# A matmul with rotary embedding: earlier first stores, half of the middle stores on another queue, two more block pairs, and a slice of the multiplication on GpSimd

## The chip, the core and the metric

The kernel runs on one core of a Trainium2 chip. A core has five engines with a queue of instructions each: TensorE (PE; PEld is its weight load), VectorE (DVE), ScalarE (ACT), GpSimd (POOL) and SyncE (SP), which only issues DMAs. Here SyncE and ScalarE issue DMAs. Matmul results go to PSUM, eight banks of 128 x 512 fp32; everything else is in SBUF. The metric is the device time of one execution in microseconds.

## What is computed

The reference, cut to what matters (batch 16, sequence 512, hidden 768, 12 heads of 64):

```
y = np.matmul(x, weight)                      # (16, 512, 768) x (768, 768)
y = y.reshape(16, 512, 12, 64)
y1, y2 = y[..., :32], y[..., 32:]
out1 = y1 * cos[..., :32] - y2 * sin[..., :32]
out2 = y2 * cos[..., 32:] + y1 * sin[..., 32:]
out = np.concatenate([out1, out2], axis=-1).reshape(16, 512, 768)
```

All arrays are float32. The kernel multiplies in fp16 with fp32 sums.

## The kernel before

**Tiles and groups.** The 8192 rows of x are 64 tiles of 128 rows; tile i has one batch and every fourth row of it. Four tiles with the same residue r of the row number are a group g (16 groups, 0 to 15), so that one piece of cos and sin serves the whole group. The results of a group are 4 x 768 = 3072 columns, which fill six PSUM banks (`py`). A tile needs 6 chunks of 128 along the contraction, and its 768 columns lie in two banks (one piece of 512, one of 256), so it takes 12 matmuls (L291).

**How x is turned.** A matmul needs x with the contraction on the partitions. There are two ways. A *turned* tile is loaded (`load`, 384 KB, rows of 3072 bytes), cast to fp16 by ScalarE (`cast`, `xc<-xs`), transposed by six TensorE transposes (L232) into a PSUM tile `pt`, and copied to SBUF by ScalarE (`xt<-pt`). A *pair* (two neighbouring tiles, listed in `BLOCKS`) is loaded so that 32 x 32 blocks lie right (four quarters of 192 KB, in pieces of 768 bytes: two quarters are issued by SyncE, two by ScalarE), cast by ScalarE (`cast_pair`, `xd<-xb`) and transposed by one VectorE instruction (L252). Before the change, the second halves of groups 3 to 14 and the first halves of groups 5, 7, 9, 11 and 13 are pairs, 17 in all; 30 tiles are turned. Pair buffers: `NB` is 4.

**The rotary part.** A *unit* is 1024 columns of a group (three units; smaller ones in the last two groups). VectorE multiplies the unit in PSUM by cos and by the swapped and signed sin at once, into `tq` (L309, output 2 x 1024). GpSimd adds the two products, the second with its halves exchanged, into the output buffer `ov` (L320). `tq` has five buffers (two of them in the space of the raw weights, named `w_raw` in the profile), `ov` has four, one a group. `store` (L341) writes half a group (768 KB).

**The order of the work.** The order on every engine is written out by hand; semaphores are placed by `Flow.do` from the buffers that an instruction reads and writes. After tile i's matmuls the loop from L510 calls, in this order: `bturns` (VectorE transposes of pairs that begin fewer than 6 tiles ahead; fewer before tile 8), `turns` (TensorE transposes and ScalarE's copy of a tile that is 3 ahead), `casts` (ScalarE's casts up to 7 tiles ahead; 4 before tile 8, and at tile 8 the casts of tiles 12 to 15 at once), and then a store if one is due. Inside `casts`, after each cast, `pump` gives SyncE the next loads whose buffers are free by then, and ScalarE gets at most one quarter of a pair, of a pair at most `LEAD` = 12 tiles ahead and only if a pair buffer is counted free:

```
                if n < xb_used[0] + NB and i >= g * QB + 2 * h - LEAD:
                    load_quarter(pairs[n], 2 + q, "act")
```

Store k (0 or 1) of group o is issued after tile 4(o+2) + 2k for groups 0 to 10, so after tiles 8, 10, 12, 14, 16, 18 for the first three groups; nearly all by ScalarE, from group 13 on by SyncE. DMAs are issued by a queue's owner in order with its other instructions: what stands behind an issue on ScalarE waits until it is done.

Of the kernel before, what the change touches and what calls it, by code (L numbers as in the profile page):

```python
# [10 lines left out]
FP32 = mybir.dt.float32  # L11
FP16 = mybir.dt.float16
MULT = mybir.AluOpType.mult
ADD = mybir.AluOpType.add


class Flow:
# [24 lines left out]
    def do(self, e, make, reads=(), writes=(), dma=None, tick=True):  # L42
        need = {}
        for k in reads:
            for s, v in self.wrote.get(k, {}).items():
                need[s] = max(need.get(s, 0), v)
        for k in writes:
            for d in (self.wrote, self.readby):
                for s, v in d.get(k, {}).items():
                    need[s] = max(need.get(s, 0), v)  # L50
        if e == "pe":
            need.pop("pe", None)
        waits = self.settle(e, need)
        for s, v in waits[:-1]:
            self.eng[e].wait_ge(self.sem(s), v)  # L55
        i = make(self.eng[e])
        if waits:
            s, v = waits[-1]
            i.wait_op(self.sem(s), v, "sem-ge")
        name, step = (dma, 16) if dma else (e, 1)  # L60
        self.sem(name)
        at = self.count[name] + step
        if tick or dma:
            i.then_inc(self.sems[name], step)
            self.count[name] = at
            self.known[name, at] = dict(self.seen[e])
        for k in reads:
            d = self.readby.setdefault(k, {})
            d[name] = max(d.get(name, 0), at)
        for k in writes:  # L70
            self.wrote[k] = {name: at}
            self.readby[k] = {}
        return i
# [30 lines left out]
def kernel(  # L104
# [11 lines left out]
    f = Flow(nc, tc)  # L116
    do = f.do
    P = nc.NUM_PARTITIONS

    B, S, H = x.shape  # L120
    NH = int(n_heads)
    D = H // NH
# [5 lines left out]
    QB = 4  # L128
# [3 lines left out]
    LAST = NG - 1  # L132


    BLOCKS = {(g, 1) for g in range(3, 15)} | {(g, 0) for g in (5, 7, 9, 11, 13)}

    def sbuf(name, shape, dt):
        return nc.alloc_sbuf_tensor(name, shape, dt).ap()

    NX, NB, NC, NCP, NXT, NXP, NTQ, NOV = 11, 4, 5, 2, 8, 4, 3, 4  # L140

    ident = sbuf("ident", [P, P], FP16)
    cold = sbuf("cold", [P, 512], FP16)
# [1 line left out]
    csn = sbuf("csn", [P, 2, SB, D], FP32)  # L145
# [8 lines left out]
    tq_b = [sbuf(f"tq{i}", [P, 2, 1024], FP32) for i in range(NTQ)]  # L154
    w_flat = w_raw.rearrange("p t e n -> p (t e n)")
    tq_b += [w_flat[:, ts(i, 2048)].rearrange("p (j n) -> p j n", j=2) for i in range(2)]
    W_HOME = [f"wr{t}{h}" for t, h in CHUNKS]
    ov_b = [sbuf(f"ov{i}", [P, QB * H], FP32) for i in range(NOV)]
    py = nc.alloc_psum_tensor("py", [P, 6 * 512], FP32).ap()
# [2 lines left out]
    def ring(name, n, state={}):  # L162
        k = state.get((id(f), name), 0)
        state[id(f), name] = k + 1
        return k % n

    def copy(e, o, i_):
        return lambda eng: (
            eng.copy(out=o, in_=i_) if e == "act" else eng.tensor_copy(out=o, in_=i_)  # L169
        )  # L170

    def where(i):
        g, s = divmod(i, QB)
        return QB * (g // SB) + s, g % SB

    def pair_of(i):
        return i // QB, (i % QB) // 2

    def is_block(i):
        return pair_of(i) in BLOCKS  # L180

# [112 lines left out]

    ov_of = {}

    late = []

    def rope(g, u):
        c0, c1, ps, banks, adder = u  # L300
        w, r = c1 - c0, g % SB
        nh = w // D
        if adder == "dve":
            k = len(late)
            tq, keys = xs_b[k][:, 0 : 2 * w].rearrange("p (j n) -> p j n", j=2), [f"xs{k}"]
        else:
            k = ring("tq", NTQ + 2)
            tq, keys = tq_b[k][:, :, 0:w], [f"tq{k}"] + (W_HOME if k >= NTQ else [])
        do("dve", lambda eng: eng.tensor_tensor(  # L309
            out=tq.rearrange("p j (h d) -> p j h d", d=D),  # L310
            in0=ps.rearrange("p (h d) -> p h d", d=D)
            .unsqueeze(1).broadcast_to((P, 2, nh, D)),
            in1=csn[:, :, r, :].unsqueeze(2).broadcast_to((P, 2, nh, D)),
            op=MULT), reads=banks + ["csn"], writes=keys)
        if g not in ov_of:
            ov_of[g] = ring("ov", NOV)
        o = ov_of[g]

        def add():
            do(adder, lambda eng: eng.tensor_tensor(  # L320
                out=ov_b[o][:, ds(c0, w)].rearrange("p (h t d) -> p h t d", t=2, d=HD),
                in0=tq[:, 0].rearrange("p (h t d) -> p h t d", t=2, d=HD),
                in1=tq[:, 1].rearrange("p (h t d) -> p h t d", t=2, d=HD)[:, :, ::-1, :],
                op=ADD), reads=keys[:1], writes=[f"ov{o}c{c}" for c in range(c0, c1, 64)])

        if adder == "dve":
            late.append(add)
        else:
            add()

    def store(g, c0, c1, e):

        o = ov_of[g]
        b, r = where(g * QB)
        s0, s1 = c0 // H, -(-c1 // H)
        dst = out.rearrange("b (p r) h -> r p b h", r=SB)[r, :, b + s0 : b + s1]
        src = ov_b[o].rearrange("p (b h) -> p b h", b=QB)[:, s0:s1]
        if (c1 - c0) % H:
            dst = dst[:, 0, c0 - s0 * H : c1 - s0 * H]
            src = src[:, 0, c0 - s0 * H : c1 - s0 * H]  # L340
        do(e, lambda eng: eng.dma_start(out=dst, in_=src),  # L341
           reads=[f"ov{o}c{c}" for c in range(c0, c1, 64)], dma=f"ov{o}_{c0}")
# [5 lines left out]
        out=ident, in_=ident, compare_op=mybir.AluOpType.not_equal, fill=1.0,  # L348
# [3 lines left out]
    for k in order:  # L352
# [5 lines left out]
        out=csn[:, 0], in_=cos.rearrange("(p r) d -> p r d", r=SB)), writes=["cos"], dma="cos")  # L358
    do("sp", lambda eng: eng.dma_start(
        out=sin_sb, in_=sin.rearrange("(p r) d -> p r d", r=SB)), writes=["sin"], dma="sin")  # L360


    want = [(i, i) for i in range(QB, NTILE) if not is_block(i)]
    for g, h in BLOCKS:
        want += [(g * QB + 2 * h - 2.5 + 3 * q, ((g, h), q)) for q in (0, 1)]
# [41 lines left out]
    def castx(i, e):  # L407
        cast(i, e)
        xs_used[0] += 1
# [22 lines left out]
    for c in CHUNKS[3:5]:  # L432
# [5 lines left out]
        out=csn[:, 1, :, 0:HD], in_=sin_sb[:, :, HD:D]), reads=["sin"], writes=["csn1"])  # L438
    do("dve", lambda eng: eng.tensor_scalar_mul(
        out=csn[:, 1, :, HD:D], in0=sin_sb[:, :, 0:HD], scalar1=-1.0),  # L440
        reads=["sin", "csn1", "cos"], writes=["csn"])
    pump()

    state = {"cast": 4, "turn": 4, "bturn": 0, "half": 0}
    pairs = sorted(BLOCKS)

    def casts(upto):
        while state["cast"] < min(upto, NTILE):
            i = state["cast"]
            state["cast"] += 1  # L450
            if not is_block(i):
                castx(i, "act")
            elif i % 2 == 0:
                cast_pair(pair_of(i))
                xb_used[0] += 1
            pump()
            if state["half"] < 2 * len(pairs):
                n, q = divmod(state["half"], 2)
                g, h = pairs[n]
                if n < xb_used[0] + NB and i >= g * QB + 2 * h - LEAD:  # L460
                    load_quarter(pairs[n], 2 + q, "act")
                    state["half"] += 1
# [31 lines left out]
    for c in CHUNKS[3:]:  # L494
        mm0(3, c)
    rope(0, U0[2])
    turns(6)

    STORES = {}
    for o in range(LAST):  # L500
        for k in (0, 1):
            if o < LAST - 4:
                at = QB * (o + 2) + 2 * k
            elif o < LAST - 2:
                at = QB * (LAST - 2) + 2 * (o - LAST + 4) + k
            else:
                at = QB * (o + 1) + 2 * k
            STORES[at] = (o, k)

    for i in range(QB, NTILE):  # L510
        g, s = divmod(i, QB)
        us = units(g)
        done_to = (s + 1) * H
        for p in pieces(g, s):
            a, z, _, bank = p
            for c in CHUNKS:
                mm_piece(i, p, c, c == CHUNKS[0], c == CHUNKS[-1],
                         tick=c == CHUNKS[-1])
            for u in us:
                if u[1] == z:  # L520
                    rope(g, u)
        bturns(i + (B_AHEAD if i >= SETTLED else 3))
        turns(i + 1 + (T_AHEAD if i > QB + 1 else 2))
        casts(i + 1 + (C_AHEAD if i >= SETTLED else 3 if i == QB else 4))
        if i in STORES:
            o, k = STORES[i]
            store(o, 2 * H * k, 2 * H * (k + 1), "sp" if o > LAST - 3 else "act")
        if g == LAST:
            if s == 2:
                store(g, 0, H, "sp")  # L530
            if s == 3:
                store(g, H, 2 * H, "act")
# [3 lines left out]
    for k, add in enumerate(late):  # L536
        c = 3 * H + 256 * k
# [38 lines left out]
```

## Time and profile before

| | |
|---|---|
| median of three runs | 151.27 us (150.74 to 152.22) |
| the profiled execution | 151.62 us, span 149.8 us |
| TensorE busy | 141.2 us, 94% of the span |
| VectorE busy | 128.7 us, 86% |
| GpSimd busy | 112.8 us, 75% |
| ScalarE busy | 74.9 us, 50% |
| moved by DMA | 53.11 MB, mean 355 GB/s |
| stores issued by ScalarE | 26 of 768 KB, median 13.7 us to landing |

A group's line in the profile has: line, engine, operation, output and input with shapes, number of instructions, then busy microseconds and the mean in nanoseconds, then the idle time of the engine before them and what ended it. A line of the chain in order of time has the start, the duration, and the work. A line of a timeline has the start, the duration, engine and line, and in brackets the engine's idle time before and what released it; "ACTq" is ScalarE's sequencer, which issues DMAs. The span is the program's own time on the core; the execution's time is 1.8 us longer.

### The profile page before, as it was taken

The page shows a single profiled execution, that of the slowest core. Times are in us where ns is not written, and L with a number is a line of the kernel's source. Part 1 is how long each engine was busy: PE and PEld are TensorE (multiplying, and loading weights), DVE is VectorE, ACT ScalarE, POOL GpSimd, SP SyncE. Part 2 cuts the span into 40 slices and gives each one's busy share as a digit, 9 for nine tenths or more (in the row PEclk, how much of TensorE's full clock was granted, in tenths as well). Part 3 has the DMA queues.
Part 4 walks back from the last instruction along what each step waited for, and adds up shares of the span by engine and source line. Part 5 has one row for each costly group of instructions (what it writes and reads, how often), then busy time and mean ns, then how long its engine had stood idle before and what let it go on. Part 6 is the DMA issues. An engine that isn't in the chain of part 4 may idle for free.

```text
span 149.8 us, 2471 instructions
## 1 busy us (share of the span) xinstructions
PE 141.2 (94%) x972; PEld 87.7 (59%) x972; DVE 128.7 (86%) x88; ACT 74.9 (50%) x76; POOL 112.8 (75%) x60
## 2 busy tenths in 40 slices
PE   6969999999999999999999999999999999999950
PEld 2435666666676655555666667565565666676730
DVE  0154999677999999999989999899989999998890
ACT  3444768886963280843563545444696118342100
POOL 1000299966897789887989889878988698999970
PEclk9999999999999999999999999999999999999995
DMA  4999999999999999999999999999999999997574
GB/s 129 346 400 399 404 348 293 287 297 260 227 323 399 390 373 384 388 386 387 389 382 396 391 395 396 398 385 395 399 410 410 418 413 417 396 403 311 229 278 152
DMA packets 33147, 53.11 MB, mean 355 GB/s; under 512 B 2288, under 2 KB 20464, under 8 KB 33136
## 3 DMA queue, kind: packets, MB, share of 16 engines
q10 hardware_dynamic: 16752, 27.79, 50.5%
q1 hardware_dynamic: 16384, 25.17, 48.7%
q8 instruction: 7, 0.11, 0.3%
q14 instruction: 4, 0.03, 0.1%
HBM read 27.79 MB, written 25.17 MB: 353 GB/s over the span
## 4 chain that ended last, share of the span: by engine, by line
PE 86%; DMA 5%; DVE 3%; SPq 1%; ACT 1%; issue 1%; ACTq 0%; DVEq 0%
PE py L291 80%; PE pt L232 6%; DMA w_raw<-in_weight_dram 5%; DVE xs L309 1%; ACT xc L169 1%; SPq L189 1%; DVE ov L320 1%; SPq L208 1%; DVE w_raw L309 0%; DVE w_sb L169 0%; ACTq L201 0%; DVE tq L309 0%; ACT xt L169 0%; DVEq L55 0%; SPq L571 0%
## 5 line engine op out<-in xcount | busy, mean ns | idle before, releaser
L320 POOL TENSOR_TENSOR ov<-tq 128x1024 f32<-128x1024 f32 (+2 forms) x33 | 69.0, 2107 | 27.4 <-DVE tq L309 25.7
L291 PE MATMUL py<-w_sb,xp 128*128 128x512 f16 (+1 forms) x408 | 69.4, 326 | 0.0
L309 DVE TENSOR_TENSOR tq<-py,csn 128x2048 f32<-128x2048 f32 (+2 forms) x33 | 65.8, 2015 | 3.8 <-PE py L291 3.5
L291 PE MATMUL py<-w_sb,xt 128*128 128x256 f16 (+1 forms) x360 | 60.8, 323 | 1.4 <-DVE w_sb L169 1.3
L291 PEld LDWEIGHTS py<-w_sb,xp 128*128 128x128 f16 x408 | 39.3, 98 | 24.6
L291 PEld LDWEIGHTS py<-w_sb,xt 128*128 128x128 f16 x360 | 34.2, 98 | 22.8 <-DVE w_sb L169 2.8
L320 POOL TENSOR_TENSOR ov<-w_raw 128x1024 f32<-128x1024 f32 (+2 forms) x21 | 43.6, 2087 | 4.2 <-DVE w_raw L309 4.2
L309 DVE TENSOR_TENSOR w_raw<-py,csn 128x2048 f32<-128x2048 f32 (+2 forms) x21 | 41.9, 1997 | 2.4 <-PE py L291 1.9
L169 ACT COPY xt<-pt 128x768 f16<-128x768 f16 x28 | 22.3, 800 | 31.9 <-PE pt L232 21.7
L169 ACT CAST xc<-xs 128x768 f16<-128x768 f32 x30 | 26.2, 905 | 17.7 <-issue 10.2
L169 ACT CAST xd<-xb 128x1536 f16<-128x1536 f32 x17 | 27.6, 1625 | 13.8 <-issue 5.0
L252 DVE STREAM_TRANSPOSE xp<-xd 128x768 f32<-128x768 f32 x17 | 16.4, 964 | 0.9 <-ACT xd L169 0.9
L232 PE MATMUL pt<-ident,xc 128*128 128x128 f16 x180 | 15.3, 222 | 0.2 <-ACT xc L169 0.2
L232 PEld LDWEIGHTS pt<-ident,xc 128*128 128x128 f16 x180 | 12.5, 99 | 5.2 <-ACT xc L169 1.8
L394 PE MATMUL py<-cold 128*128 128x512 f16 x12 | 5.3, 614 | 1.4 <-DVE cold L345 1.4
L169 DVE CAST w_sb<-w_raw 128x768 f16<-128x768 f32 x6 | 3.4, 558 | 3.5 <-DMA w_raw<-in_weight_dram 3.5
L169 DVE COPY xt<-pt 128x768 f16<-128x768 f16 x2 | 1.1, 558 | 5.6 <-PE pt L232 5.6
L394 PEld LDWEIGHTS py<-cold 128*128 128x128 f16 x12 | 1.6, 144 | 3.6 <-issue 2.2
L169 ACT ACT_TABLE_LOAD x1 | 1.3, 1283 | 0.9 <-SPq L114 0.9
L291 PE MATMUL pt<-w_sb,xt 128*128 128x256 f16 x12 | 1.5, 272 | 0.0
L309 DVE TENSOR_TENSOR xs<-pt,csn 128x512 f32<-128x512 f32 x2 | 1.3, 680 | 0.0
L291 PEld LDWEIGHTS pt<-w_sb,xt 128*128 128x128 f16 x12 | 1.2, 98 | 0.1
(11 smaller groups left out, 3.4 us busy)
## 6 DMA issues: line engine op xcount, KB each, us to landing
out_dram<-ov ACTq DMA_DIRECT2D x26, 768.0 KB, 13.7
xs<-in_x_dram SPq DMA_DIRECT2D x30, 384.0 KB, 9.8
xb<-in_x_dram SPq DMA_DIRECT2D x34, 192.0 KB, 8.2
xb<-in_x_dram ACTq DMA_DIRECT2D x34, 192.0 KB, 10.2
out_dram<-ov SPq DMA_DIRECT2D x4, 768.0 KB, 5.1
w_raw<-in_weight_dram SPq DMA_DIRECT2D x6, 384.0 KB, 7.5
out_dram<-ov SPq DMA_DIRECT2D x1, 384.0 KB, 2.3
out_dram<-ov ACTq DMA_DIRECT2D x1, 384.0 KB, 2.3
```

The lines of the kernel that those rows point to most:

```text
L169: eng.copy(out=o, in_=i_) if e == "act" else eng.tensor_copy(out=o, in_=i_)
L189: do(e, lambda eng: eng.dma_start(out=xs_b[k], in_=x[b].rearrange("(p r) h -> r p h", r=SB)[r]), writes=[f"xs{k}"], dma=f"xs{k}")
L208: do(e, lambda eng: eng.dma_start(out=w_raw[:, t, h], in_=wv[t, h]), writes=[f"wr{t}{h}"], dma=f"w{t}{h}")
L232: do("pe", lambda eng: eng.transpose(pt[:, t, h, :], src[:, t, h, :], ident), reads=[f"xc{c}", "ident"], writes=[f"pt{k}"], tick=(t, h) == ...
L252: do("dve", lambda eng: eng.transpose(out=dst, in_=src), reads=rd, writes=[f"xp{z}"])
L291: do("pe", lambda eng: eng.matmul(ps, get(t, h), w_sb[:, t, h, a - s * H : z - s * H], start=start, stop=stop), reads=[key, f"w{t}{h}"], w ...
L309: do("dve", lambda eng: eng.tensor_tensor(out=tq.rearrange("p j (h d) -> p j h d", d=D), in0=ps.rearrange("p (h d) -> p h d", d=D) .unsque ...
L320: do(adder, lambda eng: eng.tensor_tensor(out=ov_b[o][:, ds(c0, w)].rearrange("p (h t d) -> p h t d", t=2, d=HD), in0=tq[:, 0].rearrange(" ...
L394: do("pe", lambda eng: eng.matmul(py[:, ts(b, 512)], cold[:, 0:P], cold, start=True, stop=warmed[0] < WARM - 6), reads=["cold"], writes=[f ...
```

## The change

- `BLOCKS` gains (6, 0) and (10, 0): tiles 24, 25, 40 and 41 are loaded, cast and transposed as pairs. There are 19 pairs, and 26 turned tiles.
- `NB` becomes 5. So the halves of pair (6, 0) that ScalarE issues come after the casts of tiles 12 and 13.
- In groups 3 to 9, VectorE multiplies only the first 896 columns of the third unit. After the tile's other work (`held`), ScalarE copies the last 128 columns from PSUM to a small buffer `yb`, GpSimd multiplies them, and then does the unit's addition.
- Stores of groups 0 to 10 are issued after tile 4(o+1) + 2k + min(4, 1+o): for the first three groups after tiles 5, 7, 10, 12, 15 and 17; from group 3 on as before.
- The second stores of groups 2 to 8 are issued by SyncE.

```
-    BLOCKS = {(g, 1) for g in range(3, 15)} | {(g, 0) for g in (5, 7, 9, 11, 13)}
+    BLOCKS = {(g, 1) for g in range(3, 15)} | {(g, 0) for g in (5, 6, 7, 9, 10, 11, 13)}
...
-    NX, NB, NC, NCP, NXT, NXP, NTQ, NOV = 11, 4, 5, 2, 8, 4, 3, 4
+    NX, NB, NC, NCP, NXT, NXP, NTQ, NOV = 11, 5, 5, 2, 8, 4, 3, 4
+    PART = 128
...
+    yb_b = [sbuf(f"yb{i}", [P, PART], FP32) for i in range(2)]
...
+        def times(e, y, a, z, rd, wr):
+            n = (z - a) // D
+            do(e, lambda eng: eng.tensor_tensor(
+                out=tq[:, :, a:z].rearrange("p j (h d) -> p j h d", d=D),
+                in0=y.rearrange("p (h d) -> p h d", d=D)
+                .unsqueeze(1).broadcast_to((P, 2, n, D)),
+                in1=csn[:, :, r, :].unsqueeze(2).broadcast_to((P, 2, n, D)),
+                op=MULT), reads=rd + ["csn"], writes=wr)
+
+        part = c0 == 2048 and 3 <= g <= 9
+        m = w - PART if part else w
+        times("dve", ps[:, 0:m], 0, m, banks, keys)
...
+        def rest():
+            do("act", copy("act", yb_b[y], ps[:, m:w]), reads=banks[-1:] + keys[:1], writes=[f"yb{y}"])
+            times("pool", yb_b[y], m, w, [f"yb{y}"], [keys[0] + "p"])
+            add()
...
+        if part:
+            held.append(rest)
+        elif adder == "dve":
...
-                at = QB * (o + 2) + 2 * k
+                at = QB * (o + 1) + 2 * k + min(QB, 1 + o)
...
         casts(i + 1 + (C_AHEAD if i >= SETTLED else 3 if i == QB else 4))
+        while held:
+            held.pop()()
         if i in STORES:
             o, k = STORES[i]
-            store(o, 2 * H * k, 2 * H * (k + 1), "sp" if o > LAST - 3 else "act")
+            store(o, 2 * H * k, 2 * H * (k + 1), "sp" if k and 2 <= o < 9 or o > LAST - 3 else "act")
```

More of the change, by code (lines that the diff above doesn't have):

```diff
@@ L295 @@
     ov_of = {}
-    late = []
+    late, held = [], []
     def rope(g, u):
@@ L308, in rope @@
             tq, keys = tq_b[k][:, :, 0:w], [f"tq{k}"] + (W_HOME if k >= NTQ else [])
[L309 to L314, printed above, removed]
+        def times(e, y, a, z, rd, wr):
[9 more added lines that the diff above has]
+        times("dve", ps[:, 0:m], 0, m, banks, keys)
         if g not in ov_of:
@@ L317, in rope @@
         o = ov_of[g]
+        if part:
+            y = ring("yb", 2)
+        def rest():
+            do("act", copy("act", yb_b[y], ps[:, m:w]), reads=banks[-1:] + keys[:1], writes=[f"yb{y}"])
+            times("pool", yb_b[y], m, w, [f"yb{y}"], [keys[0] + "p"])
+            add()
+        if part:
+            keys = [keys[0], keys[0] + "p"]
         def add():
@@ L323, in add @@
                 in1=tq[:, 1].rearrange("p (h t d) -> p h t d", t=2, d=HD)[:, :, ::-1, :],
-                op=ADD), reads=keys[:1], writes=[f"ov{o}c{c}" for c in range(c0, c1, 64)])
-        if adder == "dve":
+                op=ADD), reads=keys[: 2 if part else 1], writes=[f"ov{o}c{c}" for c in range(c0, c1, 64)])
+        if part:
+            held.append(rest)
+        elif adder == "dve":
             late.append(add)
```

## The prediction

> **What bounds the kernel now.** I read the page's busy shares, then the chain that ended last, then the same chain in order of time.
>
> ```profile
> PE 141.2 (94%) x972; PEld 87.7 (59%) x972; DVE 128.7 (86%) x88; ACT 74.9 (50%) x76; POOL 112.8 (75%) x60
> ...
> PE 86%; DMA 5%; DVE 3%; SPq 1%; ACT 1%; issue 1%; ACTq 0%; DVEq 0%
> ```
>
> TensorE carries 86% of the chain. Its pieces in order of time give the price of each kind of work:
>
> ```profile
> 35.53 5.85 PE py L291 x36
> ...
> 60.27 13.65 PE py L291 x84
> 73.92 0.34 PE pt L232 x6
> 74.25 1.95 PE py L291 x12
> 76.20 0.34 PE pt L232 x6
> ```
>
> A tile of 12 matmuls takes 1.95 us, and the TensorE turn of a tile (six transposes) 0.34 us. From 25.88 to 142.32 us the chain lists nothing but these two: whatever is late elsewhere is hidden. A group of four tiles lasts 7.80 us with two pairs, 8.48 us with one pair and two turned tiles. Next I read ScalarE's timeline at the place where its work stands closest to TensorE's:
>
> ```profile
> 31.69 1.71 ACT L169 CAST xc<-xs 128x768 f16<-128x768 f32 x2
> 33.30 1.58 ACT L169 CAST xd<-xb 128x1536 f16<-128x1536 f32 x1
> 34.91 0.87 ACTq L201 DMA_DIRECT2D xb<-in_x_dram  x2
> 35.82 0.46 ACTq L341 DMA_DIRECT2D out_dram<-ov  x1
> 36.33 0.80 ACT L169 COPY xt<-pt 128x768 f16<-128x768 f16 x1 [1.45 <-PE py L291]
> ...
> 45.80 2.26 ACTq L341 DMA_DIRECT2D out_dram<-ov  x1
> 48.16 1.62 ACT L169 CAST xd<-xb 128x1536 f16<-128x1536 f32 x1 [2.13 <-issue]
> ```
>
> The copy at 36.33 is xT of tile 12, done at 37.13; the three tiles from 35.53 in the chain are 11, 12 and 13, so tile 12 starts at 37.48. The slack is 0.35 us, the smallest of the kernel. The last two lines show that a DMA issue can block ScalarE: a store took 2.26 us to issue, and the next cast waited on "issue". I counted what was outstanding. Up to six ACT DMAs in flight, most issues take 0.3 to 0.6 us; with seven the next takes 0.5 to 3.5 us and ends about when the one seven places ahead lands: the store issued at 45.80 left at 48.06, the one seven ahead landed at 47.70; for four later issues 52.46 and 52.18, 54.33 and 54.58, 65.47 and 65.40, 72.03 and 71.88. The ACT queue holds about seven of these transfers (16 descriptors a DMA engine each).
>
> **The change part by part.**
>
> *Two pairs more.* Four tiles (24, 25, 40, 41) lose their TensorE turns: 4 x 0.34 = 1.35 us off the path. ScalarE loses four casts of 0.905 and four copies of 0.80 and gains two pair casts of 1.625: 3.6 us less. VectorE gains two transposes; back to back one costs 0.87 (mult at 81.69 to mult at 84.75, 3.06, less the 2.19 between two mults). The loads become 768-byte packets, 36 ns each against 121 ns for 3072 bytes: 1024 x 36 less 256 x 121 is 5.9 us a pair over 16 engines, 0.37 us, 0.74 for both.
>
> *GpSimd's 128 columns.* VectorE's mult falls from 2048 to 1792 elements. The rows:
>
> ```profile
> L320 POOL TENSOR_TENSOR ov<-tq 128x1024 f32<-128x1024 f32 x26 | 61.4, 2374 | 27.4 <-DVE tq L309 25.7 <-DMA out_dram<-ov 1.7
> L309 DVE TENSOR_TENSOR tq<-py,csn 128x2048 f32<-128x2048 f32 x26 | 58.6, 2270 | 3.5 <-PE py L291 3.5
> L309 DVE TENSOR_TENSOR tq<-py,csn 128x1024 f32<-128x1024 f32 x5 | 6.1, 1221 | 0.3
> L320 POOL TENSOR_TENSOR ov<-tq 128x256 f32<-128x256 f32 x2 | 1.4, 716 | 0.0
> ```
>
> (2270 - 1221)/1024 is 1.02 ns an element, so 0.26 us a group, 1.84 over seven. VectorE against TensorE, in effective times: two pairs with the split 3 x 2.19 + 2 x 0.87 - 0.26 = 8.05 against 7.80; one pair 7.18 against 8.48. Transposes run up to two groups ahead, so by stage the lag grows 0.25 in each of groups 4, 5, 8, 9, and shrinks in 6, 7 and from 10 on. The smallest gap between a mult's end and TensorE's next write to its banks is 1.7 us, so VectorE costs nothing; without the split's saving the lag would reach 1.0, still covered.
>
> ScalarE's copy of 128 columns has no row. Its two casts give (1625 - 905)/768 = 0.94 ns an element and 0.185 fixed, so 0.31; ends 0.185 and 0.80 (the 768-column copy), which I keep. It waits for VectorE's mult of the same unit; behind it on ScalarE stand the next tile's turn copy, the casts and a store. At this point turns are three tiles ahead, so the wait of some 2.5 us past the tile's end is covered. GpSimd's 256-output mult has no row; the nearest is the 256-output add, 0.716. Ends: 0.2 (its memset of 128x128, 0.204) and 2.37 (the full add). Per group 3 x 2.33 + 0.7 = 7.7 against 7.80 or 8.48; it just fits, and five tq buffers cover it (last rival). The bank it shares is written last in the next group, two tiles later; a second wait for it on TensorE's queue, seven times, is bounded by 0.05 us each: 0 to 0.35. I take 0.
>
> *Stores on SyncE.* Seven halves leave ScalarE, where a store's issue took 0.845 us at the median. SyncE does nothing but wait: in its queue the store follows loads that wait for casts of the same time, and GpSimd finished that half long before (50.80 for group 3, stored from 64.62 on), so it neither waits nor holds the loads behind. This begins with group 2's second half, at tile 17. Worth nothing on the path.
>
> *First stores sooner, fifth pair buffer.* Here is what I expect to cost. In program order the ACT queue gets, up to tile 7: eight pair halves (A1 to A8), as now, but with store S00 after A6 (tile 5) and S01 after A8 (tile 7), which now come at tiles 8 and 10. At tile 8, with a fifth buffer, the halves of pair (6,0) are allowed at once: A9 after the cast of tile 12, A10 after that of 13, then the pair cast, A11 and A12, and only then the xT copy of tile 12. Now only two halves and S00 stand there. Counting places: A9 needs the fourth, A4, landed (31.96); A10 needs A5 (34.65), so the pair cast moves from 33.30 to about 34.8 and ends at 36.4; A11 needs that cast and A6 (36.70), about 37.0; A12 needs S00. S00 lies in the queue behind A6; stores near 48 us landed 2.2 to 2.35 us apart, and while packets are slow (768 bytes took 50 ns and 3072 bytes 154 ns at 25 to 30 us) 16 x 0.2 = 3.3. So S00 lands at 38.9 to 40.0 and A12 is issued at about 39.3. The copy of tile 12 ends at 40.1, where TensorE wants it at 37.48: 2.6 us lost. Ends: if the queue never holds, the copy comes at 35.8, sooner than now, loss 0; if every place waits for the full landing, 3.5. I take 2.6, since the seven-place count fits five issues within 0.4 us. Later S10 and S11 meet the same full queue, but by the same count xT of tile 16 is ready at 48.1 and wanted at 48.9. From tile 18 on ScalarE carries fewer transfers than now.
>
> The early stores also take DMA time from loads: 1.94 us each at most (256 x 121 ns / 16). The pair cast at 39.32 had its data 0.84 early, others 3 to 5; VectorE needs that pair 1.7 us after its cast ends, with 2.6 more until TensorE would notice. Covered.
>
> **Sum.** -1.35 + 2.6 = +1.25. The profiled execution has a span of 149.8 and took 151.62; it becomes 151.1 and 152.9. It stood 0.35 above the median of the runs, 151.27, so I forecast **152.5**.
>
> **Rivals.**
> 1. *The queue does not hold there* (faster). The count of seven was seen only after 45 us, and some issues with seven outstanding took 0.5 us (59.26, for one). Then ScalarE is freer than now and the whole 1.35 stays: 149.9; with up to 1.2 of loss, to 151.1.
> 2. *Transfers become the bound* (no difference). The DMA row shows 9 nearly throughout, and 45 to 105 us moved 390 GB/s. A two-pair group needs 3.146 MB; at 390 GB/s that is 8.07 us, not 7.80. Groups 4 to 12 move 28.3 MB, 72.6 us; TensorE needs 71.6 after and 72.9 before. So 0.3 of the gain is left: 151.0. Against it: slices reach 410 to 418 GB/s and most pair casts had data 4.5 to 7 us early. The Trainium skill (DMA: Bandwidth & Descriptors, Where 436 GB/s comes from) goes further: transfers between HBM and SBUF are bound by about 358 GB/s a core. By that rule 53.11 MB take an estimated 148.4 us and there would be nothing to gain at all; the slices of this trace, at 380 to 418 for most of the span, do not agree.
> 3. *GpSimd falls behind* (slower). Place: groups 3 to 9. A sum's buffer is written again five units later; at group 6 the add ended at 70.19 and the next mult into that buffer began at 78.60, 8.4 us of cover. Seven groups of TensorE last 56.0 us, so it decides when GpSimd needs over (56.0 + 8.4)/7 = 9.2 a group, that is mult and waiting over 2.2 us. At 2.37 and 0.5 of waiting a group takes 9.9, 13 us behind, 5 beyond the cover: 154.9. Against it: adds follow a line in size.
>
> **How the numbers follow.** The full queue 0.55 (own range 151.6 to 153.7), the gain kept 0.27, transfers 0.08, GpSimd 0.10. The range is 149.7 to 154.0: about 0.08 of the gain-kept case lies below, and GpSimd's case and a little more above. A measurement of this kernel tells about 1% from no change (149.76 and 152.78): faster takes some two fifths of the kept gain and a rest, 0.14; slower two fifths of the full queue and GpSimd's case, 0.33; within 1%, 0.53.
>
> **What would show it.** Twenty-six turned tiles in the group of transposes instead of thirty. Right: in ScalarE's timeline, issues of 1 to 3 us between 31 and 40 us, the copy of tile 12 at about 39, and a TensorE wait of 2 to 3 us before it, the only new one; after 50 us shorter ACT issues. If TensorE shows no wait there, rival 1. If waits on x loads or a store's landing appear in groups 5 to 11, rival 2. If GpSimd's 256-output mult is over 1.5 us and VectorE waits for GpSimd, rival 3. Wrong also if the copy behind VectorE's mult delays a turn copy.

## The result and the profile after

The changed kernel takes **158.83 us** at the median (158.28 to 162.74, four runs), the kernel before, run beside it, 151.75: a ratio of 1.0446, 95% interval 1.0391 to 1.0502. It is slower by 7 us. Ratios here and below are taken over fast runs alone (the run of 162.74 is a slow one), so they are not quite the quotients of the medians. I had forecast 152.5 and a range that ended at 154.0. The profiled execution took 158.28 us with a span of 156.5.

From the page of the changed kernel: busy times, the chain that ended last, and four groups of instructions (busy microseconds, mean nanoseconds, idle time before them and what ended it).

```profile
PE 139.7 (89%) x948; PEld 85.7 (55%) x948; DVE 130.5 (83%) x90; ACT 73.4 (47%) x77; POOL 117.3 (75%) x67
...
PE 41%; DVE 21%; issue 16%; POOL 12%; DMA 4%; SPq 1%; ACT 1%; ACTq 0%; DVEq 0%; POOLq 0%
...
L340 POOL TENSOR_TENSOR ov<-w_raw 128x1024 f32<-128x1024 f32 (+2 forms) x21 | 43.5, 2087 | 11.2 <-DMA out_dram<-ov 10.4
...
L172 ACT COPY yb<-py 128x128 f32<-128x128 f32 x7 | 1.9, 266 | 13.8 <-DVE tq L315 8.0
...
L340 DVE TENSOR_TENSOR ov<-xs 128x256 f32<-128x256 f32 x3 | 3.0, 1053 | 0.0
L315 POOL TENSOR_TENSOR tq<-yb,csn 128x256 f32<-128x256 f32 x4 | 2.9, 729 | 0.0
```

TensorE's busy time fell by 1.5 us, and from the start of tile 12 to the end of group 13 it takes 88.64 us against 89.98 before: the four turns brought about what was forecast, 1.35. But its share of the chain fell from 86% to 41%. One new wait is large: GpSimd waited 10.4 us for a store (`DMA out_dram<-ov`) to land, where the kernel before has 1.7. The timeline of GpSimd shows where (start, duration, operation, and in brackets the idle time before it). First the kernel before:

```profile
110.86 2.38 POOL L320 TENSOR_TENSOR ov<-w_raw 128x1024 f32<-128x1024 f32 x1 [0.41 <-DVE w_raw L309]
...
117.58 4.70 POOL L320 TENSOR_TENSOR ov<-tq 128x1024 f32<-128x1024 f32 x2 [1.71 <-DMA out_dram<-ov]
```

Then the changed kernel:

```profile
120.26 2.36 POOL L340 TENSOR_TENSOR ov<-w_raw 128x1024 f32<-128x1024 f32 x1 [10.36 <-DMA out_dram<-ov]
122.56 7.04 POOL L340 TENSOR_TENSOR ov<-tq 128x1024 f32<-128x1024 f32 x3
```

The sum at 120.26 is unit 1 of group 11. It writes the output buffer that group 7 had, so it waits until the second half of group 7 is stored. In the kernel before, ScalarE issued that store:

```profile
96.66 1.06 ACTq L341 DMA_DIRECT2D out_dram<-ov  x1
```

It landed at 110.62, and the same sum began at 110.86: a margin of 0.24 us. Now the store is SyncE's, and the timeline of SyncE shows what stands ahead of it:

```profile
85.90 6.45 SPq L204 DMA_DIRECT2D xb<-in_x_dram  x4
92.40 3.83 SPq L192 DMA_DIRECT2D xs<-in_x_dram  x2
96.26 0.48 SPq L204 DMA_DIRECT2D xb<-in_x_dram  x1
96.78 4.00 SPq L192 DMA_DIRECT2D xs<-in_x_dram  x4
100.83 4.83 SPq L363 DMA_DIRECT2D out_dram<-ov  x2
```

Eleven loads, the last ones of x, and then two stores in one piece: (group 7, second half) issued at 100.83 and landed at 120.19, and (8, second half) landed at 124.08. TensorE, VectorE and GpSimd had kept the gain until then: TensorE ended group 12 at 117.80, against 118.83 before. From 120.26 on GpSimd adds back to back. It starts 9.4 us later than before (120.26 less 110.86), makes up 2.7 us (2.4 of them are the idle time that it had there before), and ends at 151.97 against 145.28: 6.7 us later, which is the whole difference of the spans (156.5 less 149.8).

The place that I had forecast to cost 2.6 us is quiet in this execution. The timeline of ScalarE:

```profile
31.06 2.87 ACTq L204 DMA_DIRECT2D xb<-in_x_dram  x2
...
33.96 1.59 ACT L172 CAST xd<-xb 128x1536 f16<-128x1536 f32 x1 [0.50 <-issue]
35.59 1.06 ACTq L204 DMA_DIRECT2D xb<-in_x_dram  x2
...
36.69 0.80 ACT L172 COPY xt<-pt 128x768 f16<-128x768 f16 x1 [1.13 <-PE py L294]
```

The queue blocks ScalarE once, for 2.4 of the 2.87 us, and the cast of the pair is late; then two more issues go out with seven and eight transfers outstanding in 0.4 and 0.7 us, and the copy of tile 12 ends at 37.49. Tile 12 starts at 37.63, 0.10 late.

### The profile page after: what moved, and what is told of

The parts are those of the page before. It is cut to its first block, busy times and chain, and to the rows that moved or that the text cites. A ratio compares the mean times of both kernels' runs of the same rounds, so it can differ in the third digit from the quotient of the medians.

```text
span 156.5 us, 2437 instructions
## 1 busy us (share of the span) xinstructions
PE 139.7 (89%) x948; PEld 85.7 (55%) x948; DVE 130.5 (83%) x90; ACT 73.4 (47%) x77; POOL 117.3 (75%) x67
## 4 chain that ended last, share of the span: by engine, by line
PE 41%; DVE 21%; issue 16%; POOL 12%; DMA 4%; SPq 1%; ACT 1%; ACTq 0%; DVEq 0%; POOLq 0%
PE py L294 38%; POOL ov L340 12%; DVE w_raw L315 9%; DVE tq L315 6%; DMA w_raw<-in_weight_dram 4%; PE pt L235 3%; DVE xp L255 2%; DVE ov L340 2%; ACT xc L172 1%; DVE xs L315 1%; SPq L192 1%; SPq L211 1%; DVE w_sb L172 0%; ACTq L204 0%; ACT xt L172 0%
## 5 line engine op out<-in xcount | busy, mean ns | idle before, releaser
L294 PE MATMUL py<-w_sb,xp 128*128 128x256 f16 (+1 forms) x456 | 76.2, 326 | 0.0
L315 DVE TENSOR_TENSOR tq<-py,csn 128x2048 f32<-128x2048 f32 (+3 forms) x33 | 64.6, 1980 | 5.1 <-POOL ov L340 2.7
L294 PEld LDWEIGHTS py<-w_sb,xp 128*128 128x128 f16 x456 | 44.2, 98 | 28.2
L294 PE MATMUL py<-w_sb,xt 128*128 128x256 f16 (+1 forms) x312 | 52.9, 322 | 4.1 <-DVE w_raw L315 2.7
L340 POOL TENSOR_TENSOR ov<-w_raw 128x1024 f32<-128x1024 f32 (+2 forms) x21 | 43.5, 2087 | 11.2 <-DMA out_dram<-ov 10.4
L315 DVE TENSOR_TENSOR w_raw<-py,csn 128x2048 f32<-128x2048 f32 (+3 forms) x21 | 41.1, 1959 | 5.3 <-POOL ov L340 4.2
L294 PEld LDWEIGHTS py<-w_sb,xt 128*128 128x128 f16 x312 | 29.4, 98 | 22.8 <-DVE w_raw L315 3.0
L172 ACT CAST xd<-xb 128x1536 f16<-128x1536 f32 x19 | 30.9, 1624 | 12.0 <-DVE xp L255 5.1
L172 ACT COPY xt<-pt 128x768 f16<-128x768 f16 x24 | 19.0, 800 | 24.8 <-PE pt L235 13.9
L172 ACT CAST xc<-xs 128x768 f16<-128x768 f32 x26 | 22.9, 901 | 13.3 <-DMA xs<-in_x_dram 7.4
L235 PEld LDWEIGHTS pt<-ident,xc 128*128 128x128 f16 x156 | 10.4, 98 | 5.5 <-ACT xc L172 3.1
L340 DVE TENSOR_TENSOR ov<-xs 128x256 f32<-128x256 f32 x3 | 3.0, 1053 | 0.0
## 6 DMA issues: line engine op xcount, KB each, us to landing
xb<-in_x_dram SPq DMA_DIRECT2D x38, 192.0 KB, 10.4
```

What stands on the lines that cost most here:

```text
L235: do("pe", lambda eng: eng.transpose(pt[:, t, h, :], src[:, t, h, :], ident), reads=[f"xc{c}", "ident"], writes=[f"pt{k}"], tick=(t, h) == ...
L294: do("pe", lambda eng: eng.matmul(ps, get(t, h), w_sb[:, t, h, a - s * H : z - s * H], start=start, stop=stop), reads=[key, f"w{t}{h}"], w ...
L315: do(e, lambda eng: eng.tensor_tensor(out=tq[:, :, a:z].rearrange("p j (h d) -> p j h d", d=D), in0=y.rearrange("p (h d) -> p h d", d=D) . ...
L340: do(adder, lambda eng: eng.tensor_tensor(out=ov_b[o][:, ds(c0, w)].rearrange("p (h t d) -> p h t d", t=2, d=HD), in0=tq[:, 0].rearrange(" ...
```

## The experiments

Three theories. **PLACE**: the order of SyncE's queue is the cause; a store that is given to SyncE there stands behind loads emitted ahead of it, lands late, and holds an output buffer. **TRANSFERS**: the transfers as a whole are the bound, and the late landing is their symptom. **SLICE**: GpSimd is late by its own multiplication. Each run is compared with the kernel before on the same chip; ratios carry their 95% interval.

### All second halves back on ScalarE

```diff
-store(..., "sp" if k and 2 <= o < 9 or o > LAST - 3 else "act")
+store(..., "sp" if o > LAST - 3 else "act")
```

> The changed kernel with one part undone: the second stores of groups 2 to 8 go back to ScalarE's queue. Three theories of the 10.4 us for which GpSimd waited for a store's landing at 110 us. PLACE: the second store of group 7 lay in SyncE's queue behind eleven loads (the last of x among them), was issued at 100.8 and landed at 120.2; on ScalarE it is issued at about 97 and lands by 111, the wait is under 1 us, and the turns' 1.35 us remain: 149.5 to 151.2. TRANSFERS: nineteen pairs are more than the DMA engines can carry beside the stores, the landing is late whichever queue has it: 154 or more. SLICE: GpSimd is late because of its seven multiplications: 153 or more.

151.23 us, ratio 0.9933 (0.9883 to 0.9983); span 148.4, TensorE again 86% of the chain. The 7 us are gone; the bytes, the pairs and the slice are as in the changed kernel. SLICE is hard to hold, PLACE fits.

### SyncE's stores only in groups 2 to 6

```diff
-"sp" if k and 2 <= o < 9 or o > LAST - 3 else "act"
+"sp" if k and 2 <= o < 7 or o > LAST - 3 else "act"
```

> The changed kernel with SyncE's stores of groups 7 and 8 alone back on ScalarE; those of groups 2 to 6 stay on SyncE. PLACE: as with all seven back, 149.5 to 151.2, since only these two lie behind the last loads of x. TRANSFERS and SLICE: 153 or more.

151.14 us, 0.9934 (0.9889 to 0.9980), span 148.6, and no wait for a landing. The two stores of groups 7 and 8 on SyncE are the whole loss; in the changed kernel's profile only that of group 7 is waited for.

### Without the slice

```diff
-part = c0 == 2048 and 3 <= g <= 9
+part = False
```

> The changed kernel without GpSimd's multiplication: VectorE multiplies all 1024 columns of every unit, as before; all else as changed. PLACE: GpSimd still waits about 10 us near 110 us, 156 or more. SLICE: the wait goes, 152 or less. TRANSFERS: 154 or more.

VectorE multiplies the 128 columns itself, as in the kernel before. 158.49 us, 1.0429 (1.0291 to 1.0567). SLICE falls: without it the loss stands.

### Four pair buffers

```diff
-NX, NB, NC, NCP, NXT, NXP, NTQ, NOV = 11, 5, 5, 2, 8, 4, 3, 4
+NX, NB, NC, NCP, NXT, NXP, NTQ, NOV = 11, 4, 5, 2, 8, 4, 3, 4
```

> The changed kernel with four pair buffers instead of five. In SyncE's order the second store of group 7 then stands behind five quarter loads and ahead of the last six loads of turned tiles. PLACE: it lands before 112, no wait over 2 us there, 149.5 to 152. TRANSFERS: 154 or more. SLICE: 153 or more.

159.43 us, 1.0491 (1.0350 to 1.0631). My number for PLACE missed: I expected the loss to go. Its timeline of SyncE shows why it only moved:

```profile
96.09 2.16 SPq L363 DMA_DIRECT2D out_dram<-ov  x1
98.30 1.04 SPq L204 DMA_DIRECT2D xb<-in_x_dram  x1
99.39 1.40 SPq L192 DMA_DIRECT2D xs<-in_x_dram  x2
100.83 0.76 SPq L204 DMA_DIRECT2D xb<-in_x_dram  x1
101.63 6.22 SPq L192 DMA_DIRECT2D xs<-in_x_dram  x4
107.89 1.11 SPq L363 DMA_DIRECT2D out_dram<-ov  x1
```

The store of group 7 now goes earlier and lands in time (109.58). That of group 8 has the last eight loads ahead of it, lands at 129.08, and GpSimd waits 11.8 us for it, in group 12. The fifth buffer decides which of the two stores stands behind the loads, not whether one does.

### The last loads after the stores

All seven second halves stay on SyncE; only the loads from tile 56 on are held back, in the order of the program, until the store of group 8 is in the queue.

```diff
+tail = [False]
...
+            if j == 56 and not tail[0]:
+                return
...
+            if (o, k) == (8, 1):
+                tail[0] = True
+                pump()
```

> The changed kernel with all seven stores still on SyncE, and only the order of SyncE's queue altered: the loads of tile 56 and of all that follows it wait in program order until the second store of group 8 stands in the queue. PLACE (a store comes late when it stands behind the last loads of x): both stores land by 110, GpSimd waits under 1 us for landings, the gain of the pairs is there: ratio to the kernel before 0.985 to 0.998. If seven stores are too much for SyncE's queue wherever they stand: still 1.03 or more.

151.11 us, 0.9936 (0.9886 to 0.9985). The timeline of SyncE:

```profile
92.42 4.92 SPq L363 DMA_DIRECT2D out_dram<-ov  x2
97.38 2.58 SPq L192 DMA_DIRECT2D xs<-in_x_dram  x2
...
100.87 7.06 SPq L192 DMA_DIRECT2D xs<-in_x_dram  x4
```

The same two stores, now ahead of the loads, land at 109.55 and 112.31 instead of 120.19 and 124.08. Every byte, issuer and engine is that of the changed kernel, and 7.7 us go with the order of one queue. This shows PLACE and refutes TRANSFERS.

### SyncE's stores alone, on the kernel before

```diff
-store(..., "sp" if o > LAST - 3 else "act")
+store(..., "sp" if k and 2 <= o < 9 or o > LAST - 3 else "act")
```

> The kernel before with one part of the change alone: the second stores of groups 2 to 8 on SyncE. There the store of group 8 stands behind the last six loads of turned tiles, that of group 7 ahead of them. PLACE: the store of group 8 lands at 121 to 125 where GpSimd wants it at 119.9, a wait of 1 to 5 us, ratio 1.005 to 1.03. If the loss needs the two pairs more: 0.995 to 1.005.

161.13 us, 1.0592 (1.0476 to 1.0707). The direction is as expected, the size was underrated. The timeline of SyncE:

```profile
100.08 6.70 SPq L189 DMA_DIRECT2D xs<-in_x_dram  x4
106.82 0.59 SPq L341 DMA_DIRECT2D out_dram<-ov  x1
```

With four pair buffers it is again the store of group 8, issued with nine transfers of SyncE outstanding and landing 21.2 us later, at 127.97. GpSimd waits 9.8 us, at group 12 unit 1, and here little idle time is left to catch up in: it is 8.1 us late there (128.04 against 119.91) and 7.8 us at its end.

### The two pairs and the fifth buffer alone, on the kernel before

```diff
-... | {(g, 0) for g in (5, 7, 9, 11, 13)}
+... | {(g, 0) for g in (5, 6, 7, 9, 10, 11, 13)}
-NX, NB, ... = 11, 4, ...
+NX, NB, ... = 11, 5, ...
```

> The kernel before with the two pairs more and the fifth buffer alone; stores and multiplication as before. If TensorE's four turns are all that the change is worth: ratio 0.988 to 0.995 (1.35 us). If the pairs need the slice on GpSimd, VectorE's lag shows as waits of TensorE: 0.997 to 1.01. If they need the stores moved, GpSimd waits for landings: 1.00 or more.

151.78 us, 1.0024 (0.9992 to 1.0056): nothing. TensorE did gain: from the start of tile 12 to the end of group 13 it needs 88.99 us against 89.98 before, 0.99 less (88.64 in the changed kernel). The other 0.35 went to VectorE, which began its multiplication up to 3.1 us after TensorE's end of the unit in group 10 (1.06 before); the chain runs through it from 81 to 103 us. The rest is lost behind TensorE's end: VectorE is still late in group 13 (1.00 against 0.11), so GpSimd is too, and both end their last sums side by side. Two lines of the timeline:

```profile
141.71 2.65 POOL L320 TENSOR_TENSOR ov<-tq 128x512 f32<-128x512 f32 x3
143.86 1.98 DVE L320 TENSOR_TENSOR ov<-xs 128x256 f32<-128x256 f32 x3
```

VectorE's three last sums begin while GpSimd is adding (it ends at 145.21) and take 1.98 us. In the kernel before, GpSimd ends at 145.28 just as they begin at 145.17, and they take 1.08. From TensorE's last matmul to the end of the span it is 6.6 us instead of 5.5.

### SyncE to group 6, without the slice

```diff
-part = c0 == 2048 and 3 <= g <= 9
+part = False
-"sp" if k and 2 <= o < 9 or o > LAST - 3 else "act"
+"sp" if k and 2 <= o < 7 or o > LAST - 3 else "act"
```

> The changed kernel with SyncE's stores up to group 6 only, and without GpSimd's multiplication. If VectorE's lag is covered without it, as its tally of 1.0 us against 1.7 of cover says: the same ratio as with it, 0.988 to 0.997. If the slice is needed: 1.00 or more.

152.44 us, 1.0054 (1.0015 to 1.0094), against 0.9934 with the slice (and 0.9936 in the run with the last loads held back, measured beside this one at 151.11 us). So the slice is needed: VectorE's lag reaches 3.1 us in group 10 again and the three last sums take 2.14. The profile shows a second thing, at the place of my forecast. Timeline of ScalarE, and last TensorE at tile 12:

```profile
30.93 4.18 ACTq L204 DMA_DIRECT2D xb<-in_x_dram  x2
...
35.15 1.59 ACT L172 CAST xd<-xb 128x1536 f16<-128x1536 f32 x1 [1.83 <-issue]
...
37.81 0.80 ACT L172 COPY xt<-pt 128x768 f16<-128x768 f16 x1 [1.07 <-PE py L294]
...
38.76 4.06 PE L294 MATMUL py<-w_sb,xt 128*128 128x512 f16 x24 [1.35 <-ACT xt L172]
```

Here the second load waited 3.54 us for a place, the copy of tile 12 ended 1.1 us later than in the changed kernel's profile, and TensorE waited 1.35 us. The slice begins at a later tile, so it is not the cause. Three profiles of kernels with early stores and five buffers show such a wait of TensorE (1.25 without the slice, 1.46 with the last loads held back, 1.35 here), three do not. In those three, tile 12 starts between 38.19 and 38.76; in all other profiles of this case between 36.56 and 37.63. The delay is not made up later: with the last loads held back, TensorE takes the same 88.64 us from tile 12 to the end of group 13 as the changed kernel. That called for the next two runs.

### Late first stores, SyncE to group 6

```diff
-at = QB * (o + 1) + 2 * k + min(QB, 1 + o)
+at = QB * (o + 2) + 2 * k
-"sp" if k and 2 <= o < 9 or o > LAST - 3 else "act"
+"sp" if k and 2 <= o < 7 or o > LAST - 3 else "act"
```

> The changed kernel with SyncE's second halves only in groups 2 to 6, and with the first stores at the tiles of the kernel before (groups 0 to 3 leave two to four tiles later than in the changed kernel). Two theories on the early stores. QUEUE: they fill ScalarE's DMA queue before tile 12. In the profiles so far the second load issued near 31 us took 2.4 to 3.7 us with eight or nine transfers outstanding, and tile 12 began 0.1 us late in one profile and 1.4 us late in others. With late stores six or seven are outstanding there, each issue takes under 0.6 us, and tile 12 never waits: TensorE from tile 12 on is as with the early stores in their best profile, and the median falls from 151.1 to 149.8 to 150.4, ratio to the kernel before 0.985 to 0.989. FREE: the early stores cost nothing in the median and the spread of a microsecond or two comes from the start (weights), as it is in the kernel before as well: median 151.0 to 151.3, ratio 0.992 to 0.995. If early stores are needed for the buffers of the sums, GpSimd shows landing waits in groups 4 to 8 and the ratio is 0.996 or more.

**150.19 us** (149.81 to 150.5), 0.9845 (0.9795 to 0.9894); span 148.1: the best of all. ScalarE's timeline, at the same two loads:

```profile
30.63 0.82 ACTq L204 DMA_DIRECT2D xb<-in_x_dram  x2
```

Six and seven transfers are outstanding instead of seven to nine, and the two issues take 0.82 us together. With early stores the runs went from 149.85 to 151.55; here they end at 150.5. QUEUE fits. That the slower ones of those runs are the ones with the wait at tile 12 is argued from three profiles, not shown run by run, and the two intervals just touch. Neither this run's profile nor that of its partner with early stores (span 148.6) has the wait; they differ by 0.46 us, all of it before tile 12, and where that comes from is open.

### The same with every store of groups 0 to 10 on ScalarE

```diff
-"sp" if k and 2 <= o < 7 or o > LAST - 3 else "act"
+"sp" if o > LAST - 3 else "act"
```

> As the run before, with every store of groups 0 to 10 on ScalarE as in the kernel before: what is left of the change is the two pairs, the fifth pair buffer and GpSimd's 128 columns. It tells what SyncE's stores of groups 2 to 6 are worth. My prediction gave them nothing on the path: ratio within 0.003 of the run before (QUEUE: 0.985 to 0.991). The other theory (RELIEF): without them ScalarE's queue is full later, at tiles 16 to 40, issues of 1 to 3 us make its turn copies and GpSimd's slice late, and the ratio is 0.004 or more above the run before, with a TensorE wait of over 0.3 us in groups 4 to 9. Against the two pairs and the buffer alone (1.0024) it also tells what the 128 columns bring: 1.0 to 1.4 us if VectorE's lag at the end of the program (1.0 us, and three last sums of 1.98 us in place of 1.09) is their doing, nothing if not.

151.62 us (150.93 to 152.8), 0.9938 (0.9902 to 0.9975): 1.43 us slower than the run before, and its fastest run is slower than the slowest of that one. From the start of tile 12 to the end of group 13 TensorE takes 90.49 us, against 88.64 in the run before. RELIEF is right: with late first stores, SyncE's stores in groups 2 to 6 are worth 1.4 us. Timeline of ScalarE and TensorE in group 6:

```profile
65.53 1.13 ACTq L363 DMA_DIRECT2D out_dram<-ov  x1
66.76 1.58 ACT L172 CAST xd<-xb 128x1536 f16<-128x1536 f32 x1 [2.73 <-issue]
...
68.78 0.27 ACT L172 COPY yb<-py 128x128 f32<-128x128 f32 x1 [0.44 <-ACT xd L172]
...
69.10 3.09 PE L294 MATMUL py<-w_sb,xp 128*128 128x512 f16 x15 [1.25 <-ACT yb L172]
```

With seven transfers outstanding ScalarE is held by one issue after another (59.03 to 62.28, 64.05 to 66.66). The pair's cast comes late, and behind it the slice's small copy out of PSUM, and TensorE, which wants to write that bank again, waits for the copy. With early stores the same stores on ScalarE showed no such wait (the first experiment, 0.9933); why the order of the first stores matters 30 us later was not followed up.

## Why the prediction was wrong

The runs put the parts on a ladder, each rung one edit:

| edit | ratio after it | this rung, of 152 us | forecast |
|---|---|---|---|
| two pairs, fifth buffer | 1.0024 | +0.4 | -1.35 |
| GpSimd's 128 columns | 0.9938 | -1.3 | 0 |
| SyncE's stores, groups 2 to 6 | 0.9845 | -1.4 | 0 |
| early first stores | 0.9934 | +1.4 | +2.6 |
| SyncE's stores, groups 7 and 8 | 1.0446 | +7.8 | 0 |

A rung is the difference of two ratios, each known to about half a per cent (0.8 us), so of the small ones little more than the sign is sure; only the rung from 0.9938 to 0.9845 was measured within one set of runs, and the kernel before had medians of 151.75 to 152.67 us in the sets. The rung of the slice leans on that: the medians on its two sides are 151.78 and 151.62. For its worth the pair 152.44 without and 151.11 with it, measured side by side, is firmer, and so are the traces: without it TensorE loses 0.35 us to VectorE, and 1.0 to 1.1 more are lost after TensorE's last matmul. The order of the rungs matters too: with early stores, SyncE's stores in groups 2 to 6 brought nothing (0.9933 without, 0.9934 with).

**The step that failed** is "Stores on SyncE ... Worth nothing on the path": a term put at 0 that measured 7.7 us. Its reasons were half the question: that the half was finished long before, and that SyncE "neither waits nor holds the loads behind". I asked what the store does to the loads behind it, and not what the loads ahead do to the store, nor who waits for its landing. The trace of before had all of it: the landing of the store of group 7 at 110.62, GpSimd's sum at 110.86, and a wait of 1.7 us for the next one. A margin of 0.24 us was to be moved to a queue with eleven loads in it. I weighed the moved step by its issue (0.845 us at the median); its price was its place: it was issued 4.2 us later (100.83 against 96.66) and took 5.4 us longer from there to land, 9.6 in all (120.19 against 110.62).

The Trainium skill (DMA: Bandwidth & Descriptors, Issuing engines are not separate DMA queues) says that issuing from several engines only saves the sequencer's time to initiate the DMA, since all run on the same DMA engines. By that rule these edits can only help. The 7.7 us between the changed kernel and the same with two stores on ScalarE say otherwise. Its section Queues, rings and completion order, that a row's descriptors are consumed in ring order, agrees with what the held-back loads showed.

**The full queue** was the right mechanism with the wrong size. The place, tile 12, and the cause, ScalarE blocked by an issue while a pair's cast and tile 12's copy stand behind it, are in three of six profiles; but TensorE waited 1.25 to 1.46 there, 0.10 in the changed kernel's own profile. The count of seven was too strict at that time: eight and nine were taken, and the store of group 0 landed at 37.38 instead of 38.9 to 40.0. In groups 4 to 10, where I had counted, it holds only roughly: in the last experiment 17 of 24 ScalarE issues between 45 and 105 us with seven outstanding took 0.65 us or more, but one with five outstanding took 2.5.

**The two pairs** saved TensorE's turns as forecast (88.64 us against 89.98 from tile 12 to the end of group 13). "VectorE costs nothing" held with the split: in the changed kernel at least 1.27 us were left between a multiplication's end and TensorE's next write to its banks. But "without the split's saving the lag would reach 1.0, still covered" is wrong: the lag was to be paid back in groups 6 and 7, and it grew from 0.5 in group 3 to 2.3 in group 6, fell only to 1.6 in group 7, and reached 3.1 in group 10, where 0.06 us were left to TensorE's next write; and what is left of a lag in the last group is covered by nothing, since GpSimd and VectorE end the program.

**GpSimd's slice** was priced well: 0.729 to 0.732 us against 0.716, the copy 0.266 against 0.31. "It just fits" holds. The bound of 0 to 0.35 for the second wait on its bank held in the changed kernel (0) and not in the last experiment (TensorE's weight load waited 2.1 us for the slice's copy, in two pieces).

**The rivals.** No TensorE wait at tile 12 was to be the sign that the queue does not hold there: three of the six profiles with early stores and five buffers show none, so the queue holds in some profiles and not in others. GpSimd fell behind at group 11, not in 3 to 9, and by a landing, not its own work. That "waits on x loads or a store's landing appear in groups 5 to 11" was to be the sign of transfers as the bound; the sign came, but the kernel with the last loads held back moves the same bytes in 151.11 us. One wait can be the sign of a rate or of an order; only the queue's own order tells which.

## What to carry to other kernels

Before a store is moved to another queue, write down what is ahead of it there at that tile, when it will land, and which instruction writes its buffer next: the store's landing, not its issue, is what others wait for. Loads that were emitted far ahead cost nothing here until a store was put behind them; emit the store first, or leave it where the queue is short. A gain on the bounding engine is worth what the last engines to end can also give; look at their lag in the last group.

## What was not expected of the hardware

- A sum on VectorE can wait for GpSimd's sums. VectorE's three last 128x256 sums took 0.41 us each in the run with late first stores and SyncE to group 6, where GpSimd had nearly ended. In the changed kernel the first of them began at 149.91, beside three sums of GpSimd, took 2.33 us and ended 0.28 us after GpSimd's last; the other two took 0.41. With SyncE's stores alone on the kernel before, all three ran beside GpSimd's and took 0.94 to 0.98. The Trainium skill (Trainium Architecture — The Big Picture, What this means for kernel authors) says that VectorE and GpSimd contend for a shared port pair of SBUF, and that it is an exclusive lock; a sum that ends only after GpSimd's agrees.
- A 768 KB store took from its issue to its landing mostly 10 to 15 us in mid-kernel, up to 19.4 on ScalarE near 100 us, 19.4 to 22.4 behind SyncE's last loads, and 3.4 near the end with nothing outstanding on either queue.
- How many transfers ScalarE's queue takes is not one number: nine with an issue time of 1.3 us near 37 us, eight with 0.5 near 29 us, and five to eight from 50 to 100 us with waits of up to 4.2 us for the next.
